# Attention layer on one core: probability buffers by size, gate weights in halves, activations kept on chip

## The chip, the cores and the metric

The kernel runs on one core of one Trainium2 chip. The metric is device time in microseconds (us). Three runs of the kernel before took 2953.64, 2962.36 and 2976.06 us, median 2962.36. The engines are TensorE (PE; its weight loads PEld), VectorE (DVE), ScalarE (ACT), GpSimd (POOL) and SyncE (SP); SP and ACT issue the DMAs. Each engine takes its instructions in the order in which they stand in its own stream, and waits where one is not ready.

## The reference

One transformer layer on 2048 latent tokens and 256 context tokens, width 1024. Two attention branches read the same modulated input through one projection; each has a SiLU gate, and a sigmoid gate merges them.

```python
h = x * (1.0 + scale) + shift                   # context tokens likewise
p = h @ w_in                                    # cq, ckv, kr, gate_a, dq, dk, dv, gate_d, merge
# MLA branch: 8 heads, keys of 96 (64 + 32 rotary), values of 64
o_a = softmax(q_mla @ k_all.T * MLA_SCALE) @ v_all
# differential branch: 4 heads, two maps of 64, values of 128
o_d = (softmax(q1 @ k1.T) - lam * softmax(q2 @ k2.T)) @ dv_all
o_d = rms_norm(o_d) * (1 - lam_init)
y_a = (o_a * silu(gate_a)) @ w_oa;  y_d = (o_d * silu(gate_d)) @ w_ob
y = (sigmoid(m_a) * y_a + sigmoid(m_d) * y_d) @ w_out
out = layer_norm(ALPHA * x + gate * y)
```

## The kernel before

The kernel has three stages. The **front** (0 to about 937 us) builds the modulated activations `hT` in five blocks (256 context tokens, then four blocks of 512 latents), each value as a high and a low part, and projects them; every product of such pairs is three matmuls (`mm3`, L113 to L116). It keeps the activations of two latent blocks at a time. Those of blocks 3 and 4 it writes to device memory (`hT_s`, eight DMAs of 1 MB), because 21 of the 24 gate tiles of these blocks are left for later. `residual_gate` and `value_scale` are short chains of small operations on DVE, ACT and PE.

The **attention stage** (937 to 2540 us) goes through 96 units of 256 queries: 32 of the differential branch (kind 1) and 64 of MLA (kind 0), one and two in turn. Each unit has two query tiles of 128. For each, PE makes scores `ps`, DVE takes them out of PSUM (`s`, L675), ACT takes the exponential (L688), and `transposed` (L694) turns the probabilities: ACT casts them to the high half of an fp16 tile `hl` (L700), POOL subtracts for the low half (L701), and SP issues a DMA transposition into `pt` (L702). The 18 key tiles go in two buffers: 9 and 9 in the differential branch, 5 and 9 in MLA, whose other four go through PE (`px`, L707, and ACT's and DVE's copies, L709 and L710). All `hl` buffers come from one pool of four of the whole size; a short one uses part of a buffer. The product with the values (`po`) follows some units later.

Between the units stands a **filler** (`gate_units`, L618): the gate tiles that were left. It loads the activations of a block again (`fhT`), and for each gate tile two pieces of weights of FK = 4 contraction tiles: a load (`fraw`, L614), ACT's cast and POOL's subtraction (`fw`, L107 and L110), 12 matmuls into `pf`; then a tanh (`fo`) and a store. `fill` adds 0.46 or 0.6 of a tile per unit.

The **tail** (2540 to 2963 us) does the gated output projections in 8 blocks of 256 tokens (`py`, with `gated` preparing the next block's operands: `od`, `g` and `ab` loads, `pss`, `prow`, `uf`, `u`), and then the last projection `pz` with the layer norm.

The order of all this is not written out by hand. The program is recorded with priorities and a scheduler places each instruction on its engine's stream by its own simulation; the filler has the lowest priority. Pools on the right side of the on-chip memory are opened and closed in turn, so the filler's pools and the tail's first pools use the same memory.

Of the kernel before, what the change touches and what calls it, by code (L numbers as in the profile page):

```python
# [44 lines left out]
FK = 4  # L45
# [18 lines left out]
def layer_kernel(ctx: ExitStack, tc: tile.TileContext, x, c, ctxt, c_ctx, w_mod, b_mod, w_in,  # L64
# [16 lines left out]
    hT_s = [dram(f"hT{b}", [P, 2, KT, 512], F32) for b in range(2)]  # L81
# [77 lines left out]
    wi = w_in.rearrange("(j p) n -> p j n", p=P)  # L159

    with ExitStack() as st:
# [91 lines left out]
        def build_h(bi, xt, jj):  # L253
# [4 lines left out]
            h = (hp if lat else hp0).tile([P, 2, 2, n], F32R, tag=f"hT{slot}_{jj}", name=f"hT{bi}_{jj}")  # L258
# [259 lines left out]
        def value_scale(kind):  # L518
            vm = bt.tile([P, 256], F32, tag="t", name="vm")
            dve.tensor_reduce(vm[:, 0:1], vmax[:, kind, :], axis=mybir.AxisListType.X, op=ALU.max)  # L520
            pvm = ps_t.tile([1, 512], F32, tag="pt", name="pvm")
# [4 lines left out]
            dve.tensor_copy(vrow[:, 1:2], vrow[:, 0:1])  # L526
            pvb = ps_t.tile([P, 512], F32, tag="pt", name="pvb")
# [4 lines left out]
        def residual_gate():  # L532
            for hf in range(2):
                ga = tp.tile([P, 512], F32, tag="t", name="ga")
                for q in range(4):
# [3 lines left out]
                    for j in range(KT):  # L539
                        if j == 0:  # L540
                            dve.tensor_scalar(gq, wmt[:, j, :], sc[:, j, 0:1], None, op0=ALU.mult)
                        else:
                            dve.scalar_tensor_tensor(gq, wmt[:, j, :], sc[:, j, 0:1], gq, op0=ALU.mult, op1=ALU.add)
                pg = ps_t.tile([1, 512], F32, tag="pt", name="pg")
# [7 lines left out]
        def run(tiles, blocks, ups=()):  # L552
            ups = list(ups)
            cn = normed(ups[0]) if ups else None
            for _ in paired(tiles, blocks):
                if ups:
# [8 lines left out]
        residual_gate()  # L565
        run(tiles_gates(), (1, 2))
        run(tiles_c(), (3, 4))

        for bi, jj in ((b, j) for b in (3, 4) for j in range(4)):
            with tc.issue_after(last_x[0]):  # L570
                rdma(hT_s[bi - 3][:, :, 2 * jj:2 * jj + 2, :], hts[bi][jj])
# [3 lines left out]
        value_scale(1)  # L575
        run(qk[4:] + tiles_gates()[NG:], (3, 4))
        value_scale(0)


    with ExitStack() as st:  # L580
# [13 lines left out]
        fh = st.enter_context(tc.tile_pool(name="fh", bufs=4, side="right"))  # L594
        fr = st.enter_context(tc.tile_pool(name="fr", bufs=FB, side="right"))
# [22 lines left out]
        def gate_units():  # L618
            ws = []
            for b in range(2, 4):  # L620
                hs = []
                for jj in range(4):
                    h = fh.tile([P, 2, 2, 512], F32R, tag="h", name="fhT")
# [242 lines left out]
        for _ in filler:  # L866
            pass
# [208 lines left out]
```

## Time and profile before

| | us |
|---|---|
| median of three runs | 2962.36 |
| the profiled execution | 2964.99 |
| its span, first to last instruction | 2963.2 |
| PE busy | 2761.3 (93%) |
| DVE, POOL, ACT busy | 1777.4, 1522.9, 1446.5 |
| mean granted clock of PE | 0.967 |

Busy time is the time in which an engine runs an instruction; issuing a DMA is not counted. PE is busy for 93% of the span, and the busy shares of the other engines are 60% and less. The share says nothing on where the 7% lie: that takes the waits by stage. The granted clock is the share of PE's full 2.4 GHz; at 0.5 PE runs at 1.2 GHz.

### The profile page before, as it was taken

Reading aid. Unit: us, or ns where it says so; the run is one execution under the profiler, and the core shown is the slowest. Engines: PE = TensorE matmul, PEld = TensorE weight load, DVE = VectorE, ACT = ScalarE, POOL = GpSimd, SP = SyncE. Lnnn points to the kernel's source line nnn. Section 1 sums busy time; section 2 is a strip of 40 time slices with the busy share of each in tenths; the row PEclk is TensorE's granted clock in tenths of the full one; section 3 lists DMA queues with packets and bytes.
Section 4 is the critical chain, followed back from the end, with each engine's and each line's share of the span. In section 5 each row is a group of like instructions: output and inputs, shape, how many; then the busy total and the mean of one; then the engine's idle time right before and its main releaser. Section 6 shows DMA issues by size and latency. Waiting matters only on the chain. (4 is left out here: it accounts for less than half of the span.)

```text
span 2963.2 us, 44826 instructions
## 1 busy us (share of the span) xinstructions
PE 2761.3 (93%) x16049; PEld 2210.5 (75%) x16049; DVE 1777.4 (60%) x3663; ACT 1446.5 (49%) x1885; POOL 1522.9 (51%) x1018
## 2 busy tenths in 40 slices
PE   7999999999999999989989889999899889889998
PEld 5888888879777776766767667767667666789886
DVE  4476310023655777767767667677677689675454
ACT  3333222233324776766767667677677576322110
POOL 2443122232445666648657577566586555464344
PEclk9999999999999999999999999999999998899999
DMA  8467533364568999999999999999999998877542
GB/s 254 123 191 214 175 97 97 92 217 134 144 190 231 198 176 193 190 216 185 192 179 205 220 191 195 181 198 185 208 188 188 194 201 153 238 214 215 180 146 82
DMA packets 1142307, 538.39 MB, mean 182 GB/s; under 512 B 819178, under 2 KB 1091264, under 8 KB 1142084
## 3 DMA queue, kind: packets, MB, share of 16 engines
q1 hardware_dynamic: 1018376, 430.04, 66.0%
q10 hardware_dynamic: 123708, 105.49, 15.1%
q8 instruction: 126, 2.06, 0.3%
q14 instruction: 97, 0.79, 0.1%
HBM read 224.16 MB, written 118.30 MB: 116 GB/s over the span
## 5 line engine op out<-in xcount | busy, mean ns | idle before, releaser
L701 POOL TENSOR_TENSOR hl<-s,hl 128x1152 f16<-128x1152 f32 (+1 forms) x378 | 784.6, 2092 | 440.6 <-ACT hl L700 408.7
L674 PE MATMUL ps<-k,q 96*128 96x512 f32 (+3 forms) x3200 | 822.3, 391 | 25.0 <-DVE s L675 21.8
L674 PEld LDWEIGHTS ps<-k,q 96*128 96x128 f32 (+1 forms) x3200 | 546.1, 193 | 145.2 <-DVE s L675 38.4
L688 ACT ACTIVATE s<-s,z 128x2304 f32<-128x2304 f32 x256 | 567.3, 2217 | 48.4 <-DVE z L681 23.2
L700 ACT CAST hl<-s 128x1152 f16<-128x1152 f32 (+1 forms) x384 | 375.5, 1007 | 362.0 <-DMA pt<-hl 197.2
L675 DVE TENSOR_SCALAR_CACHE_REDUCE s<-ps,z 128x768 f32<-128x768 f32 (+1 forms) x512 | 450.4, 880 | 104.8 <-PE ps L674 84.3
L675 DVE TENSOR_SCALAR_CACHE_REDUCE s<-ps 128x1024 f32<-128x1024 f32 x256 | 312.1, 1219 | 129.7 <-PE ps L674 106.2
L114 PE MATMUL pp<-hT,w 128*128 128x512 f32 (+1 forms) x896 | 349.4, 392 | 5.1 <-DVE qa L333 2.8
L115 PE MATMUL pp<-hT,w 128*128 128x512 f32 (+1 forms) x896 | 350.6, 392 | 0.3 <-DVE hT L268 0.3
L116 PE MATMUL pp<-hT,w 128*128 128x512 f32 (+1 forms) x896 | 349.8, 391 | 0.0
L110 POOL TENSOR_TENSOR w<-raw,w 128x512 fp32r<-128x512 f32 (+1 forms) x126 | 164.2, 1310 | 356.1 <-ACT w L107 339.7
L724 PE MATMUL po<-pt,vd 128*128 128x256 f16 x1728 | 236.3, 279 | 21.0 <-DMA pt<-hl 20.9
L724 PEld LDWEIGHTS <-vd 128*128 128x128 f16 x1728 | 158.8, 100 | 88.1 <-issue 66.0
L737 PE MATMUL po<-pt,va 128*128 128x256 f16 x1152 | 171.6, 288 | 37.3 <-DMA pt<-hl 34.2
L114 PEld LDWEIGHTS pp<-hT,w 128*128 128x128 f32 x896 | 169.9, 190 | 45.0 <-DVE qa L333 3.2
L115 PEld LDWEIGHTS pp<-hT,w 128*128 128x128 f32 x896 | 170.0, 190 | 38.9 <-POOL hT L268 0.9
L116 PEld LDWEIGHTS pp<-hT,w 128*128 128x128 f32 x896 | 169.8, 189 | 38.4
L787 DVE SCALAR_TENSOR_TENSOR s<-s,w 128x2304 f32<-128x2304 f32 x64 | 183.5, 2867 | 0.1
L1010 PE MATMUL pz<-wz,yt 128*128 128x512 f32 x768 | 179.6, 396 | 0.8 <-DVE z L1013 0.8
L710 DVE TENSOR_TENSOR pt<-px,pt 128x512 f16<-128x512 f32 x128 | 87.8, 686 | 147.4 <-ACT pt L709 146.9
L737 PEld LDWEIGHTS <-va 128*128 128x128 f16 x1152 | 103.7, 102 | 95.9 <-issue 67.6
L1010 PEld LDWEIGHTS pz<-wz,yt 128*128 128x128 f32 x768 | 144.2, 188 | 35.8 <-DVE z L1013 1.3
(227 smaller groups left out, 4724.1 us busy)
## 6 DMA issues: line engine op xcount, KB each, us to landing
raw<-in_w_in_dram SPq DMA_DIRECT2D x122, 256.0 KB, 3.2
fraw<-in_w_in_dram ACTq DMA_DIRECT2D x79, 256.0 KB, 4.1
xt<-in_x_dram SPq DMA_DIRECT2D x32, 512.0 KB, 5.4
mg<-gt SPq DMA_DIRECT2D x64, 256.0 KB, 3.9
q<-dq ACTq DMA_DIRECT2D x60, 256.0 KB, 4.7
gt<-o SPq DMA_DIRECT2D x54, 256.0 KB, 2.0
gt<-fo ACTq DMA_DIRECT2D x42, 256.0 KB, 3.6
kn<-kst SPq DMA_DIRECT2D x36, 256.0 KB, 3.3
```

The costliest lines, as they stand in the source:

```text
L114: pe.matmul(ps, wh, mh, start=first, stop=False)
L115: pe.matmul(ps, wh, ml, start=False, stop=False)
L116: pe.matmul(ps, wl, mh, start=False, stop=last)
L674: pe.matmul(ps[:, c0:c1], qa, ka[:, c0:c1], start=(i == 0), stop=(i == len(qk) - 1))
L675: dve.tensor_scalar(s[:, k0:k0 + nk], ps, -scale, 3e38 if g == 0 else z[:, g - 1:g], op0=ALU.mult, op1=ALU.min, accum_out=z[:, g:g + 1])
L688: mark[0] = act.activation(s, s, AF.Exp, bias=b, scale=-1.0, accum_out=zsum).ins
L700: act.copy(hl[:, :, 0], se)
L701: (dve if shared and e else pool).tensor_tensor(hl[:, :, 1], se, hl[:, :, 0], op=ALU.subtract)
L724: pe.matmul(po, vv[:, w, kt, :], pt_part(pts, kt, l), start=(kt == 0 and i == 0), stop=(kt == NKT - 1 and i == 2))
L737: pe.matmul(po, vv[:, kt, :], pt_part(pts, kt, 0), start=(kt == 0), stop=(kt == NKT - 1))
L787: dve.scalar_tensor_tensor(sa, sb, w[:, 2:3], sa, op0=ALU.mult, op1=ALU.add)
L1010: pe.matmul(pz[:, n, :], y[:, yy, k, :], wz[k][ww][:, n * 512:(n + 1) * 512], start=(k == 0 and i == 0), stop=(k == KT - 1 and i == 2))
```

## The change

Five things are changed.

- `hl` tiles get two tags by size: four buffers of 9 key tiles and two of 5, where there were four of 9 for both.
- The filler's weights come in pieces of FK = 2 contraction tiles: 168 pieces of 128 KB and six matmuls instead of 84 of 256 KB and twelve. The raw weights have two buffers (of half the size), the split ones still one.
- The activations of block 4 live in a pool that stays open into the attention stage. Only block 3 is written out (four DMAs of 1 MB) and read back (16 of 256 KB) into the same tiles; the filler takes block 4 first.
- `residual_gate` and `value_scale` are generators, run in steps between tiles of the projections; both value scales run side by side.
- `gated` in the tail is a generator too: its loads stand ahead of a block, its steps after each of the block's tiles 1 to 6.

```diff
-FK = 4
+FK = 2
@@
-    hT_s = [dram(f"hT{b}", [P, 2, KT, 512], F32) for b in range(2)]
+    hT_s = dram("hT", [P, 2, KT, 512], F32)
@@
+    fst = ExitStack()
+    fh = fst.enter_context(tc.tile_pool(name="fh", bufs=1, side="right"))
@@ build_h
-            h = (hp if lat else hp0).tile([P, 2, 2, n], F32R, tag=f"hT{slot}_{jj}", name=f"hT{bi}_{jj}")
+            h = ((fh if slot == 2 else hp) if lat else hp0).tile([P, 2, 2, n], F32R, tag=f"hT{slot}_{jj}", name=f"hT{bi}_{jj}")
@@ run
-        def run(tiles, blocks, ups=()):
-            ups = list(ups)
+        def run(tiles, blocks, ups=(), small=()):
+            ups, small = list(ups), iter(small)
             cn = normed(ups[0]) if ups else None
             for _ in paired(tiles, blocks):
+                next(small, None)
...
-        residual_gate()
-        run(tiles_gates(), (1, 2))
+        run(tiles_gates(), (1, 2), small=residual_gate())
         run(tiles_c(), (3, 4))
-        for bi, jj in ((b, j) for b in (3, 4) for j in range(4)):
+        for jj in range(4):
             with tc.issue_after(last_x[0]):
-                rdma(hT_s[bi - 3][:, :, 2 * jj:2 * jj + 2, :], hts[bi][jj])
+                rdma(hT_s[:, :, 2 * jj:2 * jj + 2, :], hts[3][jj])
...
-        value_scale(1)
-        run(qk[4:] + tiles_gates()[NG:], (3, 4))
-        value_scale(0)
+        scales = [value_scale(kind) for kind in (1, 0)]
+        run(qk[4:] + tiles_gates()[NG:], (3, 4), small=zip(*scales))
+        for vs in scales:
+            for _ in vs:
+                pass
@@ attention stage, pools
-        fh = st.enter_context(tc.tile_pool(name="fh", bufs=4, side="right"))
-        fr = st.enter_context(tc.tile_pool(name="fr", bufs=FB, side="right"))
+        fr = st.enter_context(tc.tile_pool(name="fr", bufs=2, side="right"))
@@ gate_units
-            for b in range(2, 4):
-                hs = []
-                for jj in range(4):
-                    h = fh.tile([P, 2, 2, 512], F32R, tag="h", name="fhT")
+            for b in (3, 2):
+                hs = hts[4] if b == 3 else []
+                for jj in range(4 - len(hs)):
+                    h = fh.tile([P, 2, 2, 512], F32R, tag=f"hT2_{jj}", name="fhT")
...
@@ transposed
-                hl = p16.tile([P, 9, 2, P], F16, tag="hl", name="hl")[:, :n]
+                hl = p16.tile([P, n, 2, P], F16, tag=f"hl{n}", name="hl", bufs=4 if n == 9 else 2)
@@ end of the attention stage
         for _ in filler:
             pass
+    fst.close()
@@ tail
-            nxt = gated(0)
+            nxt = []
+            for _ in gated(0, nxt):
+                pass
...
-                us, nxt = nxt, (gated(b + 1) if b < 7 else None)
+                us, nxt = nxt, []
+                prep = gated(b + 1, nxt) if b < 7 else iter(())
+                next(prep, None)
...
                     rdma(y_s[b][:, t, :], y)
+                    if 1 <= t < 7:
+                        next(prep, None)
```

What the scheduler makes of it shows in the streams. Line numbers after the change are higher by 4 to 16.

**SP, opening of the attention stage** (`fhT` are the filler's activations, `dq` and `gt` stores of the front, `q` the second unit's queries). Before:

```order
L145 DMA dq_81<-st 64x2x512 x2
L422 DMA gt<-o 128x512
L608 DMA fhT<-hT_60 128x512 x7
L422 DMA gt<-o 128x512
L608 DMA fhT<-hT_60 128x512 x9
L422 DMA gt<-o 128x512 x2
L614 DMA fraw<-in_w_in_dram 128x4x128
```

and now:

```order
L145 DMA dq_80<-st 64x2x512 x4
L426 DMA gt<-o 128x512 x5
L623 DMA fraw<-in_w_in_dram 128x2x128
L617 DMA q_8493<-dq_77 64x4x256 x2
L623 DMA fraw<-in_w_in_dram 128x2x128 x2
L710 DMA_TRANSPOSE pt<-hl 128x18x128 x2
```

The sixteen loads of activations are gone from SP's stream there.

**ACT, end of the attention stage** (`wo` are the tail's weights, `od` and `oa` stores of results, `u` the tail's operands). Before, from the last but one exponential on:

```order
L688 ACTIVATE s,zs_194<-s,z 128x2304
L709 CAST pt<-px 128x4x128
L718 DMA od<-o 128x256
L909 ACTIVATE s_24082<-od 128x512
L700 CAST hl<-s 128x5x128
L700 CAST hl<-s 128x9x128
L107 CAST u<-uf 128x256 x2
L700 CAST hl<-s 128x5x128
L700 CAST hl<-s 128x9x128
L709 CAST pt<-px 128x4x128
L121 ACT_TABLE_LOAD
```

and now, after the last probabilities (`fw` are the filler's weights, `fo` and `gt` a finished gate tile and its store):

```order
L107 CAST fw_21433<-fraw 128x256
L623 DMA fraw<-in_w_in_dram 128x2x128
L107 CAST fw_21445<-fraw 128x256
L623 DMA fraw<-in_w_in_dram 128x2x128
L107 CAST fw_21457<-fraw 128x256
L623 DMA fraw<-in_w_in_dram 128x2x128
L107 CAST fw_21469<-fraw 128x256
L653 ACTIVATE fo<-pf 128x512
L656 DMA gt<-fo 128x512
L623 DMA fraw<-in_w_in_dram 128x2x128
```

The filler's pieces now stand at the end of the stage, one after another, ahead of the preparation of the tail's first block; before they were through far ahead of it.

**PE, from the last piece of the filler into the tail**, now (`pss` and `prow` prepare the first block, `py` are its projections):

```order
L115 MATMUL pf<-fhT,fw_22090 128x512
L116 MATMUL pf<-fhT,fw_22091 128x512
L921 MATMUL pss<-ones,s_24383 128x1 x4
L921 MATMUL pss<-ones,s_24389 128x1 x4
L944 MATMUL prow<-ident,zx 128x128 x8
L114 MATMUL py<-u,wo_24330 128x256 x4
```

On PE 906 of the 1008 filler matmuls stand ahead of the last scores, 24 between the last products with the values, and 78 behind them without any other matmul in between. The preparation `pss` and `prow` and the first `py`, which before stood between the last products, follow them.

## Rows read from the trace of the kernel before

**Rows 1.** Busy time by stretch; columns: stretch, length, engines (instructions), clock, DMA share, GB/s:

```profile
0.00:937.00 937.00, 893.55 (x4750) 742.70 (x4751) 365.13 (x675) 276.69 (x525) 311.40 (x269) 0.98 0.56 167
937.00:2540.00 1603.00, 1473.90 (x8767) 1112.48 (x8766) 1174.71 (x2485) 1098.57 (x1220) 1011.96 (x555) 0.96 1.03 192
2540.00:2963.00 423.00, 393.86 (x2536) 355.27 (x2534) 237.57 (x504) 71.21 (x141) 199.56 (x195) 0.97 0.57 175
```

**Rows 2.** PE's waits, 940 to 2530 us; columns: total us, times, longest:

```profile
PE po L737 <- DMA pt<-hl: 31.1, 8, 6.6
PE ps L674 <- DVE s L675: 21.8, 22, 3.4
PE po L724 <- DMA pt<-hl: 20.9, 15, 4.8
PE px L707 <- DVE pt L710: 19.7, 7, 8.7
PE pf L116 <- POOL fw L110: 9.6, 6, 3.2
PE pf L114 <- ACT fw L107: 7.2, 4, 4.9
```

**Rows 3.** ACT's waits, attention stage:

```profile
ACT hl L700 <- DMA pt<-hl: 197.2, 82, 10.8
```

**Rows 4.** Timeline, 1929 to 1932.5 us; in brackets the idle time before:

```profile
1929.90 0.72 ACT L700 CAST hl<-s 128x640 f16<-128x640 f32 x1 [10.77 <-DMA pt<-hl]
```

**Rows 5.** Groups by form, attention stage; columns: busy, mean ns, idle before by releaser:

```profile
L700 ACT CAST hl<-s 128x1152 f16<-128x1152 f32 x256 | 288.4, 1149 | 282.8 <-DMA pt<-hl 131.6 <-DVE s L787 124.2 <-DVE s L675 5.4
L700 ACT CAST hl<-s 128x640 f16<-128x640 f32 x128 | 92.3, 721 | 79.2 <-DMA pt<-hl 65.6 <-DMA k<-kn 8.0 <-POOL hl L701 2.3
```

**Rows 6.** PE's waits, front:

```profile
PE ps L674 <- ACT o L419: 2.9, 1, 2.9
```

**Rows 7.** Single lines; columns: count, ns min/median/max, first and last start, forms:

```profile
L107 ACT CAST fw<-fraw x84: 601/614/627, 936.6 to 2342.7; 128x512 fp32r<-128x512 f32 x84
L107 ACT CAST cn<-cf x42: 388/406/416, 95.4 to 836.5; 128x256 fp32r<-128x256 f32 x42
L110 POOL TENSOR_TENSOR cn<-cf,cn x42: 724/744/1184, 95.9 to 839.1; 128x256 fp32r<-128x256 f32 x42
L614 ACTq DMA_DIRECT2D fraw<-in_w_in_dram x79: 379/391/1279, 994.7 to 2308.3; - x79
```

**Rows 8.** DMA issues: count, KB each, median us to landing:

```profile
fraw<-in_w_in_dram ACTq DMA_DIRECT2D x79, 256.0 KB, 4.1
q<-qn ACTq DMA_DIRECT2D x62, 128.0 KB, 4.1
g<-gt SPq DMA_DIRECT2D x8, 1024.0 KB, 9.7
```

**Rows 9.** PE's timeline, end of the attention stage:

```profile
2514.55 0.95 PE L674 MATMUL ps<-k,q 96*128 96x512 f32 x3
2542.15 0.44 PE L114 MATMUL py<-u,wo 128*128 128x256 f32 x1
```

**Rows 10.** Two stretches: the filler's instructions, then line 688's (two an exponential):

```profile
1934.00:2030.00 96.00, 21.58 (x82) 14.97 (x82) 0.00 (x0) 1.76 (x3) 1.00 1.09 196
2433.00:2521.00 88.00, 0.00 (x0) 0.00 (x0) 0.00 (x0) 0.00 (x0) 0.88 0.84 158
1934.00:2030.00 96.00, 36.79 (x32) 1.00 1.09 196
2433.00:2521.00 88.00, 34.33 (x30) 0.88 0.84 158
```

**Rows 11.** PE's waits, tail:

```profile
PE prow L933 <- DVE ms L918: 6.2, 3, 3.8
PE prow L933 <- DVE uf L946: 4.7, 2, 3.0
PE pss L910 <- ACT s L909: 3.7, 2, 2.2
```

More of the change, by code (lines that the diff above doesn't have):

```diff
@@ L520, in value_scale @@
             dve.tensor_reduce(vm[:, 0:1], vmax[:, kind, :], axis=mybir.AxisListType.X, op=ALU.max)
+            yield
             pvm = ps_t.tile([1, 512], F32, tag="pt", name="pvm")
@@ L526, in value_scale @@
             dve.tensor_copy(vrow[:, 1:2], vrow[:, 0:1])
+            yield
             pvb = ps_t.tile([P, 512], F32, tag="pt", name="pvb")
@@ L534, in residual_gate @@
                 ga = tp.tile([P, 512], F32, tag="t", name="ga")
+                yield
                 for q in range(4):
@@ L543, in residual_gate @@
                             dve.scalar_tensor_tensor(gq, wmt[:, j, :], sc[:, j, 0:1], gq, op0=ALU.mult, op1=ALU.add)
+                yield
                 pg = ps_t.tile([1, 512], F32, tag="pt", name="pg")
@@ L619, in gate_units @@
             ws = []
-            for b in range(2, 4):
-                hs = []
-                for jj in range(4):
-                    h = fh.tile([P, 2, 2, 512], F32R, tag="h", name="fhT")
+            for b in (3, 2):
+                hs = hts[4] if b == 3 else []
+                for jj in range(4 - len(hs)):
+                    h = fh.tile([P, 2, 2, 512], F32R, tag=f"hT2_{jj}", name="fhT")
                     for l in range(2):
                         for a in range(2):
-                            ldma(h[:, l, a, :], hT_s[b - 2][:, l, 2 * jj + a, :])
+                            ldma(h[:, l, a, :], hT_s[:, l, 2 * jj + a, :])
                     hs.append(h)
-                    if b > 2:
-                        yield LOADC
-                if b == 2:
+                    yield LOADC
+                if b == 3:
                     ws.append(gate_weights(0, 0))
@@ L641, in gate_units @@
                                 (hs[j // 2][:, 0, j % 2, :], hs[j // 2][:, 1, j % 2, :]), j == 0, j == KT - 1)
-                    if (b, t) != (3, NG - 1):
+                    if (b, t) != (2, NG - 1):
                         ws += [gate_weights((t + 1) % NG, j0) for j0 in range(0, FB * FK, FK)]
@@ L897, in layer_kernel, with gated @@
             ps_r = s1_.enter_context(tc.tile_pool(name="e1pr", bufs=1, space=PSUM))
-            def gated(b):
+            def gated(b, us):
                 cs = slice(b * 256, (b + 1) * 256)
@@ L904, in gated @@
                 rdma(gt, gt_s[:, 0:KT, cs])
+                yield
                 pss = ps_r.tile([P, 512], F32, tag="r", name="pss")
@@ L922, in gated @@
                 dve.tensor_tensor(r, r, cd, op=ALU.mult)
-                us = []
                 for k in range(KT):
                     if k % 2 == 0:
+                        yield
                         pr = ps_r.tile([P, 2, 256], F32, tag="r", name="prow")
@@ L949, in gated @@
                     us.append(u)
-                return us
             def wo_half(hf):
```

## The prediction

> **What bounds the kernel now.** I read three views in turn: busy time by stretch, then the waits of TensorE (PE), then the waits of the engine that PE's waits lead back to. By stretch [rows 1], the front takes 937 us with PE busy for 893.55, the attention stage 1603 us with PE busy for 1473.90, the tail 423 us with PE busy for 393.86. So PE is the bound throughout, and what a change can win is its idle time, 43, 129 and 29 us, and what the lower clock costs. In the attention stage the mean granted clock is 0.96: 0.04 of 1603 us is 64 us of clock, against 129 us idle. That is 0.5 us of clock for each us of idle, and I price every us of idle there at 1.5 us.
>
> PE's waits in that stage [rows 2] name four things: transposed probabilities that have not landed (po on pt<-hl, 31.1 + 20.9), scores that VectorE (DVE) has not taken out of PSUM (21.8), the one PSUM buffer of the PE transposes (px, 19.7), and the filler's weights (pf, 9.6 + 7.2). Together 110.3 us. Most lead back to ScalarE (ACT): it waits 197.2 us in 82 waits for a transposition to free one of the four hl buffers [rows 3]. One row shows the chain [rows 4]: at 1929.90 a 128x640 cast has waited 10.77 us, and behind it on ACT stood the px copy that DVE needed and DVE's answer that PE needed. By form [rows 5], 131.6 us of this wait stand before the whole casts (1152 columns) and 65.6 before the short ones (640).
>
> **The change part by part.** The profiled execution took 2965.0 us, the median of the three runs is 2962.4; the sum is a difference on the former and I apply it to the latter.
>
> *Opening of the attention stage.* Sixteen loads of 256 KB leave SP's queue and four of eight 1 MB writes go. No PE wait names them; the scores' first wait there is 2.9 us [rows 6]. Between 0 and -8 with its neighbours; I take -3. The residual gate's generator moves nothing on PE or DVE, and the value scales only stand closer together: 0.
>
> *Buffers by size.* Before, each cast waits for the fourth transposition before it. Now a whole cast waits for the fourth whole one before it, which in the alternation of whole and short casts is 1 to 4 transpositions earlier; a short cast inside the MLA units waits for the same one as before. So I expect the wait of the whole casts, two thirds of ACT's 197.2 us, to go and the rest to stay. What this gives PE is bounded by 0 (the transpositions land no earlier, and PE waits for them itself) and by two thirds of the 110.3 us: 73.5 us idle, 110 us with the clock. The waits for pt<-hl are 52.0 of the 110.3 and need the landing itself, so I take half: 36.8 idle, -55 us.
>
> *Half-sized pieces.* 84 casts of 0.614 become 168 of 0.406 (price of the equal-sized cn cast): 51.6 to 68.2, +16.6 us on ACT. 80 more issues on ACT's queue at 0.391 add 31.3 [rows 7]. ACT carries 48 us more beside its 1098.57 busy of 1603. None of it is PE's if ACT's idle time covers it, all of it if not; PE's waits on ACT directly are few (7.2 of 110.3), so I take a fifth: +10. GpSimd (POOL) gets about as much work as before. The pieces' own waits are 16.8 us in 84 pieces, 0.20 each; they stay the same in sum (0) or double (+16.8, +25 with the clock). I take a third, +8. The loads: 256 KB land in 4.1 us and 128 KB on the same queue in 4.1 [rows 8], so halving a load does not halve its latency; in the stage two raw buffers hide it. The Trainium skill ("DMA: Bandwidth & Descriptors", Bandwidth) speaks against such a split: batch DMAs to 1 MiB, since each carries about 2.0 us of fixed cost; by that rule 84 more loads would be an estimated +168 us if each lay on the path, where I put 0 for the loads.
>
> *Where the filler stands.* PE's order decides this. Before, all 1008 filler matmuls are through at about 2348 us. Now 102 of them stand behind the last scores, and the last 78, thirteen pieces, have no other PE work between them. A piece has one weight buffer and two raw ones, so pieces alone run in a ring: the cast 0.41, the subtraction 0.74, the next issue 0.39, a landing of 4.1 [rows 7, 8], for two pieces in flight: 5.6/2, about 2.8 us a piece; by cast, subtraction and the three matmuls of a piece that need the lower weight part (0.26 us of PE time each, 21.58 us for 82 [rows 10]) alone about 1.9. Thirteen pieces are 25 to 37 us; I take 35. In addition the first loads of the tail (od, g) reuse memory of the filler's activations and stand behind it: g lands in 9.7 us [rows 8], and before all of this lay under the end of the attention stage, where 27.6 us pass from the last scores to the first output projection [rows 9]. Between 3 and 15 us bare; I take 10. Against it, 102 matmuls leave the rest of the stage. At 0.26 us each that is 27 us if PE alone set the pace; but 16 exponentials with 82 filler matmuls took 96.0 us and 15 without any 88.0 [rows 10], 93.9 for 16, so a filler matmul costs as little as 0.03 us where other engines set it. Between -3 and -27; I take -16, since the stretch without filler ran at clock 0.88. Together +29, bounds +1 to +49.
>
> *Tail.* The preparation of the next block is spread over the projections. PE's waits for it are 6.2 + 4.7 + 3.7 = 14.6 us [rows 11]. PE's order there is nearly the same as before, so I take half: -8, bounds 0 and -22.
>
> Sum: -3 -55 +10 +8 +29 -8 = -19. That is 2946 for the profiled execution and **2943 us** for the median.
>
> **The rivals.**
> *The ring does all it can.* PE loses the whole 73.5 us: -110 in place of -55, sum -74, 2888. For it: the filler waits and px sit behind the same ACT wait. Against: the longest wait shown is a short cast, whose buffer is no freer than before.
>
> *The transfers are the limit.* The DMA engines' busy share in the stage is 1.03 [rows 1]. Then ACT's wait turns into PE's own wait for the same transpositions, the ring gives 0, and ACT's extra work hides under it: -3 +29 -8 = +18, 2980. Against: the stretch of 96.0 us ran at clock 1.00 and a DMA share of 1.09 [rows 10]. The Trainium skill ("Trainium Kernel Development and Optimization", Key Constraints) says that DMAs from all queues run on the same 16 engines and interleave, which speaks for this rival: a longer queue of transpositions gets no more bandwidth. The trace agrees in that the waiting cast of [rows 4] ended only when the DMA did.
>
> *Slower: the short pieces run dry.* A piece lasts six matmuls, then its cast needs ACT, its subtraction POOL and both need their turn in engines that carry the probabilities. If a piece waits 0.42 us on the mean instead of 0.20, 168 pieces idle PE for 70.6 us, 48 more than the 22.4 in my sum (16.8 + 5.6), +73: sum +54, 3016. It decides from about 0.33 us a piece, where the sum passes +29. For it: waits of whole pieces took 9.6 + 7.2 us already, and the end shows thirteen pieces with no cover. Against: the scheduler has put other PE work between most pieces.
>
> That part of the change does nothing holds for the residual gate and is in the sum at 0.
>
> **How the numbers follow.** About 1% is what a measurement of this kernel can tell from no change. My forecast has 0.42, reaching some 35 us to both sides (0.18 faster by over 1%, that is under 2933; 0.19 within; 0.05 slower); the full ring 0.26, all faster; the transfers 0.15 (0.12 within, 0.03 slower); the dry pieces 0.17, slower. Faster 0.44, within 1% 0.31, slower 0.25. Cases of both signs hold most of the chance: the forecast's own range is 2908 to 2978. The range goes to 2880, just past the full ring, and to 3012, just short of the dry pieces; about 0.1 lies outside at either end.
>
> **What would show it.** ACT's wait for pt<-hl before whole casts falls under 40 us and before short ones stays near 65. PE's idle in the attention stage falls from 129 to about 100. After the last scores stand some 13 pieces 2 to 3 us apart, and the first projection comes 60 to 75 us after the last scores, not 27.6. Waits on pf above 60 us in sum, or an unchanged ACT wait, would make me wrong.

## The result, and the profile after

| | before | changed |
|---|---|---|
| median of 20 runs, us | 2960.59 | 2973.65 |
| lowest to highest | 2946.38 to 2976.06 | 2954.55 to 2984.61 |
| the profiled execution | 2964.99 | 2966.81 |
| ratio to before, 95% interval | | 1.0052 [1.0033, 1.0070] |

The change makes the kernel slower by 0.52%, some 15 us. That is less than the 1% that the prediction counts as no change, but it is clearly on the other side of zero from my forecast of -19; it lies inside the range. The two profiled executions lie only 2 us apart. In the changed kernel's 20 runs the time falls by 22 us for each 0.01 of mean granted clock (correlation -0.75), so one pair of profiles shows where time goes, and the ratios show how much.

Busy time by stretch, the changed kernel; the cuts are the last projection of the front, the last scores, the first and the last output projection of the tail. Columns as in [rows 1].

```profile
0.00:923.10 923.10, 879.97 (x4745) 737.58 (x4746) 364.07 (x674) 275.56 (x525) 316.46 (x274) 0.99 0.55 161
923.10:2453.40 1530.30, 1411.65 (x8516) 1059.65 (x8514) 1132.24 (x2404) 1073.84 (x1242) 998.11 (x604) 0.97 1.05 191
2453.40:2525.30 71.90, 51.19 (x256) 33.21 (x254) 20.46 (x46) 28.74 (x52) 19.19 (x21) 0.90 0.80 203
2525.30:2773.30 248.00, 222.02 (x1767) 215.99 (x1768) 156.46 (x333) 57.40 (x121) 124.43 (x141) 0.96 0.69 203
```

The kernel before, cut at the same events:

```profile
0.00:931.70 931.70, 891.17 (x4741) 741.06 (x4742) 362.64 (x670) 274.96 (x521) 310.75 (x268) 0.98 0.56 166
931.70:2515.10 1583.40, 1459.43 (x8670) 1101.86 (x8669) 1160.26 (x2450) 1083.39 (x1199) 1006.43 (x550) 0.96 1.03 191
2515.10:2542.20 27.10, 19.06 (x120) 13.44 (x118) 16.94 (x40) 16.90 (x25) 6.18 (x5) 0.69 1.13 250
2542.20:2771.50 229.30, 211.95 (x1754) 209.81 (x1754) 144.97 (x295) 54.23 (x112) 116.74 (x132) 0.97 0.73 216
```

The first two stretches are 62 us shorter, the next two 64 us longer. In the attention stage PE has 154 matmuls less to do, 102 of them the filler's, which have moved behind it; its idle time is 118.65 us where it was 123.97. So nearly all of the 53 us there is work that went elsewhere, and clock.

ACT's wait for transpositions in the attention stage, which answers to [rows 3] and [rows 5]; first the sum:

```profile
ACT hl L708 <- DMA pt<-hl: 78.3, 44, 7.3
```

and by form:

```profile
L708 ACT CAST hl<-s 128x1152 f16<-128x1152 f32 x254 | 284.7, 1150 | 172.5 <-DVE s L795 34.8 <-DMA pt<-hl 34.3 <-DVE s L683 26.5
L708 ACT CAST hl<-s 128x640 f16<-128x640 f32 x126 | 90.9, 722 | 65.7 <-DMA pt<-hl 44.0 <-PE ps L682 6.8 <-DMA fraw<-in_w_in_dram 3.5
```

The whole casts' wait went from 131.6 to 34.3 us, as forecast; the short ones' fell too, from 65.6 to 44.0, where I had them stay near 65. PE's waits in the same stretch, which answer to [rows 2]:

```profile
PE po L732 <- DMA pt<-hl: 36.4, 17, 9.0
PE pf L114 <- ACT fw L107: 21.8, 9, 8.8
PE px L715 <- DVE pt L718: 19.5, 4, 9.6
PE po L745 <- DMA pt<-hl: 15.0, 2, 8.2
PE pf L114 <- ACT fo L653: 4.7, 2, 3.4
PE ps L682 <- DVE s L683: 3.9, 7, 1.2
```

ACT waits 119 us less for transpositions, but its idle time in the stage falls by 44 us only (500.0 to 456.5), since other waits take the place; and PE's falls by 5. PE's own waits for the transpositions did not move (between these cuts 54.1 us before and 53.6 now, a third and smaller row included), nor did the one for px. PE's waits before scores went from 24.9 to 3.9 us, and the waits on pf rose from 19.5 to 30.8.

PE's timeline behind the last scores: start, duration, instruction, in brackets the idle time before.

```profile
2487.73 0.50 PE L114 MATMUL pf<-fhT,fw 128*128 128x512 f32 x1 [0.26 <-ACT fw L107]
...
2490.06 0.50 PE L114 MATMUL pf<-fhT,fw 128*128 128x512 f32 x1 [0.26 <-ACT fw L107]
...
2510.51 0.40 PE L116 MATMUL pf<-fhT,fw 128*128 128x512 f32 x1
2516.08 1.87 PE L921 MATMUL pss<-ones,s 128*128 128x1 f32 x8 [5.17 <-ACT s L920]
...
2525.33 1.22 PE L114 MATMUL py<-u,wo 128*128 128x256 f32 x4 [0.75 <-ACT u L107]
```

Thirteen pieces, 2.33 us from one to the next in the two shown, then 14.4 us from the last of them to the first output projection. That one comes 71.9 us after the last scores, within the 60 to 75 that I had.

### The profile page after: what moved, and what is told of

It reads as the page before. It is cut to its first block, busy times and chain, and to the rows that moved or that the text cites. A ratio compares the mean times of both kernels' runs of the same rounds, so it can differ in the third digit from the quotient of the medians.

```text
span 2965.0 us, 45294 instructions
## 1 busy us (share of the span) xinstructions
PE 2744.5 (93%) x16049; PEld 2190.7 (74%) x16049; DVE 1765.9 (60%) x3663; ACT 1452.5 (49%) x1967; POOL 1541.0 (52%) x1102
## 4 chain that ended last, share of the span: by engine, by line
PE 60%; DMA 19%; DVE 7%; issue 4%; ACT 4%; POOL 3%; SPq 1%; ACTq 1%; POOLq 0%; DVEq 0%
PE ps L682 13%; DMA pt<-hl 11%; PE pp L114 7%; PE pp L115 7%; PE pp L116 7%; PE pz L1026 6%; PE po L732 4%; PE po L745 3%; PE po L750 2%; PE pf L116 2%; PE pf L114 2%; PE pf L115 2%; POOL hl L709 1%; ACT s L696 1%; DMA mg<-gt 1%
## 5 line engine op out<-in xcount | busy, mean ns | idle before, releaser
L732 PE MATMUL po<-pt,vd 128*128 128x256 f16 x1728 | 247.2, 281 | 39.4 <-DMA pt<-hl 36.4
L110 POOL TENSOR_TENSOR fw<-fraw,fw 128x256 fp32r<-128x256 f32 x168 | 152.4, 907 | 199.8 <-ACT fw L107 169.8
L745 PE MATMUL po<-pt,va 128*128 128x256 f16 x1152 | 163.4, 278 | 19.5 <-DMA pt<-hl 17.0
L795 DVE SCALAR_TENSOR_TENSOR s<-s,w 128x2304 f32<-128x2304 f32 x64 | 175.1, 2737 | 0.2
```

The lines of the kernel that those rows point to most:

```text
L110: eng_lo.tensor_tensor(lo, t32, hi.bitcast(F32) if hi.dtype == F32R else hi, op=ALU.subtract)
L732: pe.matmul(po, vv[:, w, kt, :], pt_part(pts, kt, l), start=(kt == 0 and i == 0), stop=(kt == NKT - 1 and i == 2))
L745: pe.matmul(po, vv[:, kt, :], pt_part(pts, kt, 0), start=(kt == 0), stop=(kt == NKT - 1))
```

## The experiments

All times are ratios to the kernel before, run beside it on the same chip, with 95% intervals; 1% is some 30 us. Where two experiments are compared, the uncertainty is the root of the sum of squares of the two half intervals.

| | hl buffers | pieces | ratio |
|---|---|---|---|
| changed kernel | 4 whole, 2 short | half | 1.0052 [1.0033, 1.0070] |
| 1, other edits alone | 4 | whole | 0.9974 [0.9955, 0.9993] |
| 2, half-sized pieces alone | 4 | half | 1.0160 [1.0125, 1.0194] |
| 3, rings and pieces | 4 and 2 | half | 1.0079 [1.0058, 1.0100] |
| 4, changed, single ring | 4 | half | 1.0185 [1.0149, 1.0220] |
| 5, changed, whole pieces, shared buffer | 4 and 2 | whole | 1.0102 [1.0063, 1.0140] |
| 6, changed, filler's priority raised | 4 and 2 | half | 1.0025 [0.9998, 1.0051] |
| 7, changed, 3 and 3, whole pieces | 3 and 3 | whole | 0.9941 [0.9914, 0.9968] |
| 8, changed, 4 and 1, whole pieces | 4 and 1 | whole | 1.0327 [1.0298, 1.0355] |
| 9, changed, 3 and 3 | 3 and 3 | half | 1.0016 [0.9981, 1.0051] |
| 10, as 9, two split buffers | 3 and 3 | half | 1.0003 [0.9979, 1.0026] |
| **11, before, 3 and 3** | 3 and 3 | whole | **0.9934 [0.9909, 0.9958]** |
| 12, before, two loads a piece | 4 | whole | 0.9992 [0.9966, 1.0019] |
| 13, before, two loads, two casts | 4 | whole | 1.0004 [0.9983, 1.0025] |
| 14, before, filler slower | 4 | whole | 1.0176 [1.0144, 1.0209] |
| 15, as 11, filler's priority raised | 3 and 3 | whole | 1.0153 [1.0114, 1.0192] |

No run has four whole buffers, two short ones and whole pieces with nothing else changed: experiment 5 is the nearest, and it shares a buffer besides.

**The parts of the change, one by one.** Experiment 1, the front, the kept activations and the tail's generator alone (experiments 1 and 4 to 10 are edits of the changed kernel, the others of the kernel before):

```diff
-FK = 2
+FK = 4
-        fr = ... bufs=2
+        fr = ... bufs=1
-                hl = p16.tile([P, n, 2, P], ..., tag=f"hl{n}", bufs=4 if n == 9 else 2)
+                hl = p16.tile([P, 9, 2, P], ..., tag="hl")[:, :n]
```

> The changed kernel with one ring of four whole hl buffers and with filler pieces of four contraction tiles, as before: only the front, the kept activations and the tail's generator are left of the change. In PE's order no filler matmul stands behind the last scores (102 in the changed kernel). Theory 1 (the half-sized pieces push the filler behind the last scores, and that stretch costs the 64 us that the changed kernel takes longer from its last scores to its last output projection): the stretch goes back to about 256 us, the front keeps its -9, ACT's wait for transpositions goes back to about 197; about 2950 us, 10 below before. Theory 2 (the tail's generator or the moved loads cost the end, whatever the pieces): the stretch stays above 290, about 3000 us or more, since the ring's gain is gone too.

Measured -0.26%, some 8 us. The stretch from the last scores to the last output projection is 257.4 us (256.4 before, 319.9 in the changed kernel): the other edits do not lengthen the end, and the tail's generator does not shorten it. Theory 2 falls.

Experiment 2, the kernel before with FK = 2 and two raw buffers; experiment 3, the same with the two rings:

```diff
-FK = 4
+FK = 2
-        fr = ... bufs=FB
+        fr = ... bufs=2
```

> The kernel before with half-sized filler pieces (two raw buffers) and nothing else of the change. In PE's order 96 filler matmuls stand behind the last scores. Theory 1 (place of the filler): +40 from the end (64 less the 24 that the 96 matmuls take away from the rest), and up to +19 from waits on pf: 2995 to 3020. Theory 2 (the end is the fault of the other edits): the stretch behind the last scores stays under 275 us, and the time within 1% of before. Theory 3 (pieces run dry everywhere): waits on pf over 60 us and the attention stage itself longer than before, above 3020.

> The kernel before with half-sized pieces and the two rings of hl buffers (four whole, two short), without the front's and the tail's edits. 102 filler matmuls behind the last scores. If the ring is worth what its share of the attention stage shows in the changed kernel (5 us of idle and some 15 of clock), this lies 15 to 25 us below the kernel with the half-sized pieces alone, about 2980 to 2990. If the transfers are the limit, ACT's wait falls to about 80 us and the two kernels differ by less than 8 us. If the ring does what I forecast (-55), 40 us or more below.

Half-sized pieces alone cost 1.60%, some 47 us; with the rings beside them 0.79%. So the rings are worth -0.81% with an uncertainty of 0.40, some 24 us. ACT's wait for transpositions in the two whole profiles, 2 and then 3:

```profile
ACT hl L700 <- DMA pt<-hl: 200.6, 87, 11.4
ACT hl L700 <- DMA pt<-hl: 118.9, 58, 9.4
```

The profile of experiment 2 has the end of the changed kernel, with nothing else of the change in it:

```profile
924.00:2486.90 1562.90, 1433.27 (x8507) 1067.71 (x8505) 1138.08 (x2407) 1073.33 (x1244) 1021.19 (x609) 0.96 1.02 188
2486.90:2558.30 71.40, 52.31 (x269) 33.91 (x267) 20.44 (x47) 30.79 (x54) 18.84 (x21) 0.90 0.82 209
2558.30:2807.90 249.60, 220.40 (x1768) 212.94 (x1769) 157.31 (x332) 57.20 (x121) 122.91 (x141) 0.98 0.70 202
```

and the attention stage of experiment 3:

```profile
929.40:2481.80 1552.40, 1422.25 (x8500) 1063.07 (x8498) 1140.98 (x2407) 1077.90 (x1245) 1010.36 (x609) 0.96 1.05 190
```

In experiment 2 the stretch from the last scores to the last output projection takes 321.0 us in place of 256.4, and the attention stage gives back 20.5. PE's waits on pf in the stage are 41.1 us, not over 60: the pieces do not run dry (theory 3). With the rings ACT waits 82 us less for transpositions and PE is idle as long as without them, 130.2 us and 129.6. The two profiled executions differ by 5 us only, so they do not show where the 24 us lie.

Experiment 4, the changed kernel with the one ring of four:

```diff
-                hl = p16.tile([P, n, 2, P], ..., tag=f"hl{n}", bufs=4 if n == 9 else 2)
+                hl = p16.tile([P, 9, 2, P], ..., tag="hl")[:, :n]
```

> The changed kernel with one ring of four whole hl buffers instead of two by size; everything else of the change is left in, half-sized pieces too. 66 filler matmuls behind the last scores, 36 of them bare (102 and 78 in the changed kernel). By the ring alone: ACT's wait for transpositions back to about 190 us and +20 (idle 5, clock 15) against the changed kernel; by the place of the filler -17 (42 fewer bare matmuls, seven pieces at 2.34 us). Together about 2975, equal to the changed kernel within 0.5%. If the ring is worth -55: 3000 or more. If it is worth nothing: about 2957.

1.85% over before, so here the rings are worth -1.33% (uncertainty 0.40), 39 us, although 42 fewer bare matmuls (the filler's, with no other PE work between them) stand at its end. ACT's wait for transpositions in the attention stage is 210.8 us. Against experiment 1 the half-sized pieces cost 2.11% here (uncertainty 0.40), 63 us, not 47: the parts of the change do not simply add.

**What of the half-sized pieces costs: two tries that misled.** Experiment 6 moves the filler away from the end by its priority:

```diff
-                with after(mark[0]), tc.high_priority(offset=-2000):
+                with after(mark[0]), tc.high_priority(offset=0):
```

> The changed kernel as it is, half-sized pieces too; one number is changed: the filler's instructions are recorded with the same priority as the rest, not 2000 lower. On PE all 1008 filler matmuls stand ahead of the last scores, the last of them at nine tenths or more of these. Theory 1 (what the pieces cost is mostly their place at the end): the 320 us from the last scores to the last output projection go to about 257, and the 102 matmuls return to the attention stage at up to 0.26 us each (+27): about -37 against the changed kernel, 2937. Theory 3 (half-sized pieces cost wherever they stand, by ACT's casts and issues): the attention stage grows by 60 us or more, and the time stays at 2970.

No filler stands behind the last scores, the stretch there falls to 274.7 us, and the time is only 0.27% (uncertainty 0.32) below the changed kernel: the attention stage takes 1578.9 us, 48.6 more. Read alone this says that the place is worth little. Experiment 15 makes the same edit where the filler was not late:

> The kernel before with three whole and three short hl buffers, whole pieces, and the filler's instructions recorded with the same priority as the rest. The filler is through at about nine tenths of the scores, as without the last edit. A filler matmul ahead of work that PE's queue waits for costs 0.23 us; where PE waits for transpositions it fills the gap: 2940 to 2960, no difference to the rings alone (2948) above 0.4%.

It costs 2.2% (uncertainty 0.46), some 65 us, against experiment 11, which differs in this number alone. ACT's casts in its attention stage:

```profile
L700 ACT CAST hl<-s 128x1152 f16<-128x1152 f32 x254 | 289.7, 1150 | 325.2 <-DMA pt<-hl 186.5 <-DVE s L787 80.2 <-issue 22.9
L700 ACT CAST hl<-s 128x640 f16<-128x640 f32 x126 | 90.7, 722 | 22.2 <-DMA k<-kn 8.3 <-DMA pt<-hl 6.5 <-DVE o L717 2.1
```

The whole casts wait 186.5 us for transpositions, against 55.8 in experiment 11. (In experiment 6 ACT's wait for them is 157.6 us in the stage, where the changed kernel has 78.3.) The raised priority is an edit with a large price of its own, so experiment 6 shows two things at once and its small difference proves nothing about the place.

Experiment 5 gets whole pieces beside both rings by giving the finished gate tile the raw-weight buffer:

```diff
-                    o = fo.tile([P, 512], F32, tag="fo", name="fo")
+                    o = fr.tile([P, 512], F32, tag="raw", name="fo")
```

> The changed kernel with pieces of four contraction tiles, as before, and both rings (four whole, two short). The room for it comes from the finished gate tile, which takes the filler's one raw-weight buffer instead of one of its own. No filler matmul stands behind the last scores. Theory 1 (the ring gains and the half-sized pieces lose it): -8 for the other edits, as in the kernel with these alone, and -24 to -51 for the ring, as the two pairs with half-sized pieces showed: 2902 to 2930. Theory 2 (the ring gains only where half-sized pieces load ACT): 2945 to 2955, and PE's waits on transpositions in the attention stage as in the kernel before (54). If the shared raw buffer holds up the filler, waits on pf rise over 40 us.

Slower, 1.02%, and by neither theory: PE waits 88.6 us for transpositions (54.1 before), ACT 38.4 us for the weights' loads (32.8 in experiment 7, which shares no buffer). In the program the shared buffer puts each tile's store ahead of the next load; the waits on pf stay at 9.9 us, so it did not hold up PE through the filler. What the corner of the table is worth stays open.

**The place, and the instructions alone.** Experiment 14 slows the filler's rate in the kernel before:

```diff
-FILL = (0.46, 0.6)
+FILL = (0.36, 0.47)
```

> The kernel before with whole pieces; only the filler's rate is lowered (0.36 and 0.47 of a tile per unit in place of 0.46 and 0.6), until 108 filler matmuls stand behind the last scores, 72 of them bare, as with half-sized pieces (96 and 72). If the place costs (a): the stretch from the last scores to the last output projection about 320 us, and +1% or more, 2990. If what the end loses is given back by the 108 matmuls that the attention stage no longer carries: within 0.4% of before.

+1.76%, some 52 us, with whole pieces, whole buffers and one ring. A late filler is enough to cost what half-sized pieces do. The slower rate also moves the filler within the stage, where PE is idle for 137.8 us (124.0 before), so the place does not stand quite alone here. Its stretches:

```profile
931.70:2493.40 1561.70, 1423.92 (x8535) 1073.11 (x8533) 1146.74 (x2409) 1069.36 (x1168) 1003.23 (x533) 0.96 1.02 188
2493.40:2571.50 78.10, 51.47 (x242) 37.09 (x240) 20.51 (x47) 29.44 (x47) 16.67 (x13) 0.81 0.73 188
2571.50:2823.50 252.00, 223.50 (x1767) 216.99 (x1768) 156.51 (x329) 57.05 (x120) 122.46 (x141) 0.96 0.68 199
```

The attention stage gives back 21.7 us for 108 matmuls; 51.0 are lost before the first output projection, and 22.7 behind it, where no filler stands. Experiment 2 has nearly the same parts: 20.5 given back, 44.3 and 20.3 lost. The longest waits from the first to the last output projection in experiment 14:

```profile
PE prow L933 <- DVE uf L942: 8.2, 5, 3.3
PE prow L933 <- DVE ms L918: 7.0, 3, 3.5
PE py L115 <- DVE u L110: 5.1, 8, 1.8
PE pss L910 <- ACT s L909: 4.5, 4, 1.5
PE py L114 <- ACT u L107: 4.3, 4, 1.6
```

The two py rows are new: the projections wait for their operands, 9.4 of the 11 us by which PE's idle time grows in this stretch. The other half of the 22.7 is busy time, most of it (8.4 us) in the same 1535 matmuls of the projections, at a clock of 0.96 in place of 0.97. What goes with it is the lead of the preparation. The table has how much of that PE has behind it at the first output projection (matmuls prow, 16 to a block; 24 are a block and a half), and how long the projections then take:

| kernel | prow ahead of the first py | first to last py, us |
|---|---|---|
| before | 24 | 229.3 |
| 1, 12, 13 | 16 | 238.5 to 240.7 |
| 5, 6, 7, 8, 10, 11, 15 | 8 | 242.4 to 248.9 |
| changed, 2, 3, 4, 9, 14 (filler last) | 8 | 245.8 to 252.0 |

Each half block of lead lost goes with some 9 us in this stretch. With a filler at the end the lead is small; with the larger rings it is too (experiments 7 and 11 have no filler there), and why the scheduler places it so there was not settled. No run changes the lead alone, so that it costs the time is argued and not shown: experiments 12 and 13 lose the first half block and 9 to 11 us in this stretch, and as a whole take no longer than the kernel before.

Experiment 12 doubles the loads in the kernel before, experiment 13 the casts and subtractions as well:

```diff
-            lq[0].dma_start(raw, wi[:, j0:j0 + FK, c0:c0 + P])
+            for h0 in (0, 2):
+                lq[0].dma_start(raw[:, h0:h0 + 2], wi[:, j0 + h0:j0 + h0 + 2, c0:c0 + P])
```

and in experiment 13 besides:

```diff
-            split(raw, w[0], w[1], eng_lo=pool)
+            for h0 in (0, 2):
+                split(raw[:, h0:h0 + 2], w[0][:, h0:h0 + 2], w[1][:, h0:h0 + 2], eng_lo=pool)
```

> The kernel before; each filler piece of four contraction tiles is loaded by two DMAs of 128 KB into the two halves of its one raw buffer, then cast and subtracted whole as before. Only the number of loads on ACT's queue doubles (84 more issues of 0.39 us, 33 us of ACT). No filler matmul behind the last scores. Theory C (the issues on ACT cost): +0.5% or more, 2975 or more. Theory A: within 0.3% of before.

> The kernel before with its whole buffers; each piece of four contraction tiles is loaded by two DMAs of 128 KB, cast by two casts of 128x256 and subtracted by two subtractions. ACT and POOL get every instruction of the half-sized pieces (168 loads, casts and subtractions), but PE still takes twelve matmuls from one buffer, and nothing stands behind the last scores. If the number of instructions costs (b): +0.6% or more, 2980 or more. If the small buffers (c) or the place (a) cost: within 0.3% of before.

No change in either. Experiment 13 has all the instructions of the changed kernel's filler on ACT and POOL:

```profile
L107 ACT CAST fw<-fraw x168: 388/403/417, 932.8 to 2366.8; 128x256 fp32r<-128x256 f32 x168
L110 POOL TENSOR_TENSOR fw<-fraw,fw x168: 715/733/3164, 934.4 to 2369.4; 128x256 fp32r<-128x256 f32 x168
L615 ACTq DMA_DIRECT2D fraw<-in_w_in_dram x158: 373/482/2089, 992.0 to 2355.8; - x158
```

ACT's idle time covers them, to within 0.2%.

**The rings.** Experiment 11 is the kernel before with three whole and three short buffers:

```diff
-                hl = p16.tile([P, 9, 2, P], F16, tag="hl", name="hl")[:, :n]
+                hl = p16.tile([P, n, 2, P], F16, tag=f"hl{n}", name="hl", bufs=3)
```

Experiment 7 has the same line in the changed kernel with whole pieces (FK = 4, one raw buffer), experiment 8 four and one there:

```diff
-                hl = p16.tile([P, n, 2, P], F16, tag=f"hl{n}", name="hl", bufs=4 if n == 9 else 2)
+                hl = p16.tile([P, n, 2, P], F16, tag=f"hl{n}", name="hl", bufs=4 if n == 9 else 1)
```

> The kernel before with three whole and three short hl buffers and nothing else changed. No filler matmul behind the last scores. The kernel with the front's and tail's edits alone took 0.26% less, with these rings besides 0.59% less. If the two add up: 0.33% less than before, about 2952. If the ring's worth is what the pairs with half-sized pieces showed (24 and 39 us): 2921 to 2938. If the ring only gains together with the other edits: no change.

> The changed kernel with pieces of four contraction tiles and three whole and three short hl buffers (42 key tiles of room; four whole and two short are 46, the one ring of before 36). No filler matmul behind the last scores. In the MLA units both kinds of cast have three buffers where they had two on the mean; in the differential units the whole casts have three where they had four. If the ring's gain is made in the MLA units (64 of 96): 2925 to 2940. If the loss in the differential units outweighs it: 2955 or more.

> The changed kernel with pieces of four contraction tiles, four whole and one short hl buffer (41 key tiles of room). No filler matmul behind the last scores. If what counts is the whole casts' wait, as I forecast: ACT's wait before whole casts under 40 us and 2925 to 2940. If each short cast then waits for the transposition of the short one just before it, ACT is held there: wait before short casts well over 65 us, 2960 or more.

Experiment 11 is the best kernel of the case: -0.66% against before. The other edits add nothing to it (+0.07%, uncertainty 0.36). Its casts and its attention stage with what follows:

```profile
L700 ACT CAST hl<-s 128x1152 f16<-128x1152 f32 x254 | 285.6, 1150 | 217.8 <-DVE s L787 83.3 <-DMA pt<-hl 55.8 <-issue 14.8
L700 ACT CAST hl<-s 128x640 f16<-128x640 f32 x126 | 90.9, 721 | 41.8 <-PE ps L674 12.9 <-issue 9.0 <-DMA pt<-hl 8.3
```

```profile
924.30:2474.20 1549.90, 1440.14 (x8635) 1091.99 (x8634) 1147.76 (x2432) 1079.75 (x1191) 995.89 (x545) 0.96 1.05 194
2474.20:2503.70 29.50, 16.16 (x140) 12.23 (x139) 14.49 (x24) 13.71 (x19) 3.55 (x3) 0.93 1.08 233
2503.70:2750.20 246.50, 223.22 (x1767) 217.02 (x1768) 158.56 (x330) 61.21 (x127) 122.52 (x140) 0.95 0.72 211
```

Against before, the attention stage gains 33.5 us, 14 of them idle time of PE, and the projections lose 17.2, with 8 matmuls of lead in place of 24. And experiment 8:

```profile
L708 ACT CAST hl<-s 128x1152 f16<-128x1152 f32 x253 | 283.5, 1150 | 139.8 <-DVE s L795 67.1 <-DMA pt<-hl 25.6 <-DVE s L683 16.7
L708 ACT CAST hl<-s 128x640 f16<-128x640 f32 x126 | 91.1, 723 | 218.6 <-DMA pt<-hl 201.9 <-DVE s L683 6.2 <-DVE o L725 5.7
```

Here the whole casts wait least of all, and the kernel is the slowest of all, 3.9% behind experiment 7: each short cast waits for the transposition of the one before, 201.9 us in sum, and stands on ACT ahead of everything else.

Experiments 9 and 10 put half-sized pieces on the good rings: 9 is the changed kernel with bufs=3 in that line, 10 has two split buffers as well:

```diff
-        fw = st.enter_context(tc.tile_pool(name="fw", bufs=FB, side="right"))
+        fw = st.enter_context(tc.tile_pool(name="fw", bufs=2, side="right"))
```

> The kernel with three whole and three short hl buffers that took 0.59% less than before, with pieces of two contraction tiles again (two raw buffers, one split one). 72 filler matmuls behind the last scores, 42 bare. Theory A (one split buffer: the next piece's cast stands on ACT and waits there for PE to have read the piece before, and this holds ACT as well as the filler): +0.8 to 1.6% against the kernel with whole pieces, 2968 to 2992, and ACT's wait of fw for PE's pf over 40 us. Theory B (the ring of half as much data does no harm once the short casts have their buffers): under 2955.

> As the kernel before this one, with half-sized pieces, but two split buffers. No filler matmul stands behind the last scores: the scheduler places the filler as it does whole pieces. Twice as many issues and casts on ACT remain (48 us). Theory A (one split buffer is what costs): ACT's wait of fw for pf under 20 us and the time within 0.4% of the kernel with whole pieces, 2935 to 2957. Theory C (the number of issues and casts on ACT costs): +0.8% or more, 2968 or more, though nothing stands at the end.

Against experiment 7 half-sized pieces cost 0.75% (uncertainty 0.44), and with two split buffers 0.62% (0.36). The attention stage and what follows to the last output projection, experiment 9 and then 10:

```profile
924.40:2460.50 1536.10, 1427.56 (x8517) 1063.94 (x8515) 1128.04 (x2400) 1078.40 (x1248) 1006.73 (x608) 0.96 1.03 191
2460.50:2769.50 309.00, 265.45 (x2023) 244.78 (x2022) 177.75 (x381) 84.45 (x166) 138.84 (x158) 0.95 0.73 209
933.10:2492.70 1559.60, 1437.02 (x8655) 1092.93 (x8653) 1142.06 (x2432) 1086.41 (x1270) 1007.48 (x623) 0.96 1.06 191
2492.70:2768.50 275.80, 236.37 (x1884) 225.59 (x1883) 171.28 (x349) 74.50 (x145) 126.29 (x142) 0.96 0.74 211
```

Two split buffers bring the filler back to its old place (the stretch behind the last scores is 275.8 us, 276.7 in experiment 7) and the time does not follow: 33 us less there, 24 more in the stage, and -0.13% as a whole (uncertainty 0.42). So a late filler has no fixed price: it cost 52 us in experiment 14, and here, with 72 matmuls late in place of 108, 4 us with an uncertainty of 12. That the place is what half-sized pieces cost in the changed kernel is therefore likely, by the same stretches in experiments 2 and 14, and not shown. Theory A, as I put it for these two runs, is not borne out. Theory C fits experiment 10 and not 12 and 13. What these 18 us are stays open: ACT waits 137.5 us for transpositions in experiment 10 and 72.1 in 7 within the attention stage, in an order that differs in many places.

Four pairs differ by the edit of the rings alone (the order that the scheduler makes of it moves with it). What the rings change in each, with the waits and PE's idle time of the attention stage from one profiled execution each, in us:

| without, with rings | time (uncertainty) | ACT's wait for transpositions | PE's own wait for them | PE idle |
|---|---|---|---|---|
| 2, 3 | -24 (12) | 198.8, 118.5 | 32.5, 45.0 | 129.6, 130.2 |
| 4, changed | -39 (12) | 210.8, 78.3 | 48.0, 53.6 | 138.2, 118.6 |
| before, 11 | -20 (7) | 197.2, 64.1 | 54.1, 56.0 | 124.0, 109.8 |
| 1, 7 | -10 (10) | 191.8, 72.1 | 54.8, 56.8 | 139.0, 109.7 |

ACT's wait falls by 80 to 133 us, and PE's own wait for transpositions in none.

## Why the prediction was wrong

The sum was -3 and -8 for the front and tail, +10, +8 and +29 for the pieces, -55 for the rings.

- **The rings: the step that failed.** I bounded their gain by 0 and two thirds of PE's waits, and took half with the clock, -55. Pairs that differ in the rings alone give -24 and -39 with four and two (uncertainty 12), and -20 and -10 with three and three (uncertainty 7 and 10). The first half of the mechanism was there: the whole casts' wait fell as forecast. The step from ACT's wait to PE's was not: 119 us less on ACT left PE's waits for pt<-hl at 54 us. In none of the four pairs did these waits fall, and PE's idle time in the stage fell by 0 to 29 us where I had 36.8. I had seen that these waits need the landing itself, and still took half of a bound that contained them. In the changed kernel only the waits for scores fell, and 11 us more waits on pf took half of that; PE's idle time in the stage is 119 us, not about 100. With -24 the rings are 31 of the 34 us between -19 and the +15 measured, and the front and tail the other 3. Added up by way of experiments 1 and 4, the rings (-39) are 16 and the pieces (+63) another 16: how the miss divides depends on the order, that the rings fell short does not.
- **Short casts.** I gave all the gain to the whole casts, since 131.6 of the 197.2 us stood before them. A wait before an instruction shows where the ring was short, not which of its members needs room: with four and one the whole casts hardly wait and the kernel loses 3.3%.
- **The pieces: right in sum by luck, wrong in parts.** +47 forecast, +47 measured (experiment 2), but +63 on the other edits and +22 on the better rings (experiment 9 against 7). The +10 for ACT's extra work is 0 on the kernel before (experiment 13, +0.04%, uncertainty 0.21). The +8 for the pieces' waits was too little: in experiment 2 the waits on pf rise by 22 us (19.5 to 41.1), and PE's idle time in the stage by 6, so most of that came out of other waits. For the filler's place I had +29 and no more than +49; experiment 14 gives +52. To the first projection I had 45 for the bare pieces and the cold start, and experiment 2 has 44 (experiment 14 has 51); given back I had 16, and they have 21 and 22. Behind the first projection they lose 20 and 23 us that I did not have at all, because I read the order only to the first py and not how far the preparation then ran ahead. Experiments 9 and 10 are the exception named above.
- **Front and tail.** -11 forecast, -8 measured (experiment 1, uncertainty 6), 0 on top of the better rings. The tail's -8 did not come: its stretch is as long as before, and no profile shows where the measured 8 us lie. (As a sum the -8 was a slip: half of its bound of 22 is 11, half of the 14.6 is 7.) The 8.6 us that the profiles show in the front are the clock: its idle time is 43.1 us now and 40.5 before, with the same work at 0.99 and 0.98.
- **The rivals.** The ring that does all it can (2888) is out: -10 to -39 measured, not -110. The limit by transfers gave 2980, near the 2973.65, but for another reason: it has the rings at 0, and they are not. Its sign that PE's wait takes the place of ACT's is half there, since PE's waits for transpositions stayed. For it I had counted [rows 4], which shows a cast waiting for a transposition, not that the DMA engines had no room: experiment 11 moves 194 GB/s in the stage where before had 191. The pieces that run dry did not occur: waits on pf are 36.6 us in the whole profile.

The Trainium skill ("DMA: Bandwidth & Descriptors", Bandwidth) wants transfers batched; by the fixed cost of about 2.0 us that the page gives for a DMA issued by GpSimd (Anatomy of one DMA), an estimate is 168 us for 84 more loads, were each on the path. Experiment 12 has 168 loads of 128 KB, issued by ACT and SP, in place of 84 of 256 KB, at -0.08% (uncertainty 0.27): here, off the path, they cost nothing that shows.

## What to carry to other kernels

A wait that another engine has is worth to the bound engine only what its own waits lose, and can be replaced by that engine's next wait; read both after a change, and test a ring with one buffer fewer of each size before deciding which size lacks room. Low-priority filler work is cover only as long as it ends before the work that it covers: in experiment 14 a late one lost 51 us ahead of the next stage and 23 in it, and gave back 22. So look where it ends, and count how many steps ahead the next stage's preparation stands, not only where it starts. In a kernel whose order a scheduler makes, any edit moves everything: an experiment that undoes one cause by another knob (a priority) needs the knob alone beside it.

## What was not expected of the hardware

The front is the same work in all profiles (4740 to 4745 PE instructions, 37.1 to 43.1 us idle), and it takes from 921.6 to 933.1 us, at mean granted clocks of 0.98 to 0.99. In experiment 10, which has the longest, the first 100 us ran at 0.91, where the others have 0.95 to 1.00. Between profiles of the same work some 11 us are thus mostly clock, more than the differences that the front's edits could make.
